# Gate/up projections of an f32 encoder on one core: a fourth seven-product pair per group, and the eight-product pairs' weight halves made by DMAs

## The chip, the cores and the metric

The kernel runs on one core of one Trainium2 chip. The metric is the device time of one execution in microseconds; several runs are summed up by their median. A core has TensorE (PE, matrix products), VectorE (DVE), ScalarE (ACT), GpSimd (POOL) and SyncE (SP). Each takes its own instructions strictly in order and waits on semaphores for the others. Loads from the chip's large memory (HBM) are DMAs: SP, ACT and POOL have a queue each, and all three share 16 DMA engines.

## The reference

A two-layer encoder over 256 tokens of width 2048, all in f32: in each layer a token mixer (spatial gating in the first, grouped-query attention in the second) with a memory attention beside it, an output projection, and a SwiGLU network. The change is in the last:

```python
def swiglu(h, w_gate_up, w_down):
    gate, up = jnp.split(h @ w_gate_up, 2, axis=-1)   # 2048 -> 2 x 5632
    return (jax.nn.silu(gate) * up) @ w_down          # 5632 -> 2048
```

## The kernel before

**Three passes per product.** TensorE multiplies in the rounded type F32R. To keep f32 accuracy each operand is split into an upper half, `hi` (the value rounded to F32R), and a lower half, `lo` (the value minus `hi`). One product of a 128-row slice of activations with a 128 x 512 block of weights is then three matmuls into the same PSUM bank: hi·hi, lo·hi and hi·lo (`matmul3`, lines 187 to 189). In the last the *weights'* lower half, tile `wlo`, is the moving operand. `halves` (line 265) makes a weight block's halves: ACT casts the loaded tile `raw` to `whi` (line 271), and DVE subtracts `whi` from `raw` into `wlo` (line 272). The pool has three buffers each for `whi` and `wlo`, used in turn, and four for `raw`.

**Pairs.** `Pair` (line 333) computes two 512-column blocks at once. For the gate/up projection these are a block of gate columns and the block of up columns that belongs to it; a group `f` of 11 in each layer is one such `Pair` object. The 2048 rows of the weights are eight *pairs* `i` of 256 rows. The two row slices, two token tiles and two column blocks of a pair make a 2 x 2 by 2 x 2 block product:

- `eight` does it with eight products, 24 matmuls, and needs the halves of four weight blocks (128 x 2048 in one tile);
- `seven` does it by a Strassen-like scheme with seven products, 21 matmuls. It needs sums of weights (tile `T`, three blocks, made by DVE on lines 371 to 373), the halves of seven blocks, and sums of activations (`feature_sums`, line 806), made once per layer and kept.

Products 1, 5, 6 and 7 occur in seven-product pairs alone; after the last of these `inner` (line 410 ff., the ACT copy of line 425 and the DVE adds of lines 426 to 428) combines them in tile `e`. Products 2, 3, 4 and 8 go on to the end of the group, when `outer` adds them to `e` with four DVE adds (line 448). Then ACT applies SILU (line 847) and the result is turned by DMA transposes for the down projection. In a layer's group 0 two of the eight pairs are seven-product pairs, in the other ten groups three, in the order 0, 3, 1, 4, 2, 5, 6, 7 with 0, 1 and 2 the seven-product ones.

**Order.** `run` (line 350) loads a pair (`fetch`, line 378; two DMAs of 512 KB on SP's queue) and starts its sums one pair ahead of its products. A scheduler then sets the final order of each engine's instructions, so matmuls of neighbouring pairs are interleaved. The down projection uses the same class with weights `w_down`.

## Time and profile before

| | |
|---|---|
| median of three runs | 1997.43 us (1996.91 to 1998.39) |
| the profiled execution | 2000.43 us |
| its span, first to last instruction | 1998.7 us |
| TensorE busy | 1987.4 us, 8956 matmuls |
| VectorE busy | 1595.2 us |
| ScalarE busy | 1228.9 us |
| GpSimd busy | 66.4 us |
| read from HBM | 394.45 MB |

The profile is of one execution. A row of a *group view* gives source line, engine, operation, output tile <- input tiles, form, count, then total busy time and mean ns of one, then the idle time just before them with what ended it. A row of *windows* gives a stretch of the span and, for each engine, busy us and instruction count (x), then the granted TensorE clock (1.00 is full), the mean busy share of the DMA engines (which goes a little over 1 when packets overlap) and GB/s. A row of *DMA issues* gives tile <- tensor, queue, count, size and median us from issue to landing.

### The profile page before, as it was taken

The numbers are of one execution on the slowest core, as the hardware profiler recorded it, in microseconds if no ns is written. First come the engines' busy times: TensorE is split into PE (matmuls) and PEld (weight loads), VectorE is DVE, ScalarE is ACT, GpSimd is POOL, SyncE is SP. The second block draws the span as 40 slices with busy tenths as digits, with TensorE's granted clock in tenths as the row PEclk, the third lists the DMA queues.
The fourth block names the chain that finished last, engine by engine and source line by source line (L and its number), as shares of the span: only waits on it lengthen the run. The fifth ranks groups of instructions, "written<-read, shape, count | busy, mean of one in ns | idle before, by whom it ended". The sixth has DMA issues, their size and how long they took to land.

```text
span 1998.7 us, 23974 instructions
## 1 busy us (share of the span) xinstructions
PE 1987.4 (99%) x8956; PEld 1646.0 (82%) x8956; DVE 1595.2 (80%) x1700; ACT 1228.9 (61%) x1476; POOL 66.4 (3%) x106
## 2 busy tenths in 40 slices
PE   9999999999999999999999999999999999999998
PEld 7888888888888878888888888888888888888887
DVE  6665568998888979886666886699988899888887
ACT  8757775676446764466765765756754466644673
POOL 2200001000000000000011000010000000000000
PEclk9999999999999999999999999999999999999999
DMA  9856875676656877657766434757866567765674
GB/s 352 296 187 179 242 212 188 190 231 216 220 197 183 229 201 229 205 184 232 228 219 201 162 129 158 219 180 207 241 205 212 188 206 213 225 219 190 199 220 139
DMA packets 276965, 416.48 MB, mean 208 GB/s; under 512 B 85200, under 2 KB 85456, under 8 KB 276848
## 3 DMA queue, kind: packets, MB, share of 16 engines
q1 hardware_dynamic: 199808, 387.62, 59.6%
q10 hardware_dynamic: 74352, 18.81, 5.8%
q0 software_dynamic: 2688, 8.52, 1.4%
q8 instruction: 70, 1.15, 0.2%
q14 instruction: 47, 0.39, 0.1%
HBM read 394.45 MB, written 2.10 MB: 198 GB/s over the span
## 4 chain that ended last, share of the span: by engine, by line
PE 89%; DVE 4%; DMA 3%; issue 2%; ACT 2%; SPq 0%; ACTq 0%; DVEq 0%
PE acc L189 26%; PE acc L187 26%; PE acc L188 26%; PE m L189 4%; PE m L187 4%; PE m L188 4%; DVE wlo L272 2%; DMA a<-a 1%; ACT whi L271 1%; DMA raw<-in_w_down 1%; DMA raw<-in_w_in_a 1%; PE m L193 1%; DVE T L371 0%; DVE e L448 0%; PE m L542 0%
## 5 line engine op out<-in xcount | busy, mean ns | idle before, releaser
L272 DVE TENSOR_TENSOR wlo<-raw,whi 128x2048 fp32r<-128x2048 f32 (+2 forms) x466 | 840.4, 1819 | 253.1 <-ACT whi L271 235.5
L271 ACT CAST whi<-raw 128x2048 fp32r<-128x2048 f32 (+2 forms) x466 | 705.6, 1535 | 428.5 <-PE acc L188 316.4
L187 PE MATMUL acc<-whi,h 128*128 128x512 f32 x1440 | 561.4, 390 | 0.8 <-ACT whi L271 0.8
L188 PE MATMUL acc<-whi,h 128*128 128x512 f32 x1440 | 561.0, 390 | 0.0
L189 PE MATMUL acc<-wlo,h 128*128 128x512 f32 x1440 | 516.0, 391 | 0.7 <-DVE wlo L272 0.6
L187 PE MATMUL acc<-whi,a 128*128 128x512 f32 x1052 | 410.0, 390 | 3.3 <-DVE x L448 2.1
L188 PE MATMUL acc<-whi,a 128*128 128x512 f32 x1052 | 410.0, 390 | 0.0
L189 PE MATMUL acc<-wlo,a 128*128 128x512 f32 x1052 | 394.4, 390 | 0.2 <-DVE wlo L272 0.2
L189 PEld LDWEIGHTS acc<-wlo,h 128*128 128x128 f32 x1440 | 270.4, 188 | 59.6 <-DVE wlo L272 4.1
L187 PEld LDWEIGHTS acc<-whi,h 128*128 128x128 f32 x1440 | 270.4, 188 | 56.5 <-ACT whi L271 1.5
L188 PEld LDWEIGHTS acc<-whi,h 128*128 128x128 f32 x1440 | 270.4, 188 | 55.7
L187 PEld LDWEIGHTS acc<-whi,a 128*128 128x128 f32 x1052 | 197.6, 188 | 44.7 <-issue 2.5
L189 PEld LDWEIGHTS acc<-wlo,a 128*128 128x128 f32 x1052 | 197.6, 188 | 42.3 <-DVE wlo L272 1.7
L188 PEld LDWEIGHTS acc<-whi,a 128*128 128x128 f32 x1052 | 197.6, 188 | 40.5
L271 ACT CAST whi<-T 128x1536 fp32r<-128x1536 f32 x84 | 124.4, 1481 | 96.3 <-PE acc L188 75.9
L272 DVE TENSOR_TENSOR wlo<-T,whi 128x1536 fp32r<-128x1536 f32 x84 | 146.9, 1749 | 0.0
L371 DVE TENSOR_TENSOR T<-raw 128x1024 f32<-128x1024 f32 x84 | 102.3, 1217 | 26.0 <-DMA raw<-in_w_gate_up 24.0
L189 PE MATMUL m<-wlo,a 128*128 128x512 f32 x272 | 106.1, 390 | 0.2 <-DVE wlo L272 0.2
L187 PE MATMUL m<-whi,a 128*128 128x512 f32 x272 | 106.0, 390 | 0.2 <-ACT whi L271 0.2
L188 PE MATMUL m<-whi,a 128*128 128x512 f32 x272 | 105.9, 389 | 0.0
L206 ACT COPY sg<-a 128x1024 uint16<-128x1024 uint16 x44 | 51.6, 1174 | 54.9 <-DMA a<-a 54.7
L200 ACT COPY a<-sg 128x1024 uint16<-128x1024 uint16 x44 | 45.9, 1044 | 26.0 <-issue 13.2
(122 smaller groups left out, 1474.7 us busy)
## 6 DMA issues: line engine op xcount, KB each, us to landing
raw<-in_w_gate_up SPq DMA_DIRECT2D x352, 512.0 KB, 4.7
raw<-in_w_down SPq DMA_DIRECT2D x176, 512.0 KB, 5.0
raw<-in_w_out SPq DMA_DIRECT2D x32, 1024.0 KB, 5.3
raw<-in_w_in_a SPq DMA_DIRECT2D x24, 1024.0 KB, 6.9
raw<-in_w_in_b SPq DMA_DIRECT2D x24, 1024.0 KB, 5.2
raw<-in_w_mem_kv SPq DMA_DIRECT2D x16, 1024.0 KB, 5.2
a<-in_mem_t POOLq DMA_DIRECT2D x16, 256.0 KB, 3.9
raw<-in_w_in_a SPq DMA_DIRECT2D x7, 512.0 KB, 8.1
```

What stands on the lines that cost most here:

```text
L187: nc.tensor.matmul(out, lhsT=a[0], rhs=b[0], start=start, stop=False)
L188: nc.tensor.matmul(out, lhsT=a[1], rhs=b[0], start=False, stop=False)
L189: nc.tensor.matmul(out, lhsT=a[0], rhs=b[1], start=False, stop=stop)
L193: nc.tensor.transpose(dst[:, c * P:(c + 1) * P], src[:, c * P:(c + 1) * P], ident)
L200: nc.scalar.copy(planes.rearrange("p (h n) -> p h n", h=2), src.bitcast(U16).rearrange("p (n h) -> p h n", h=2))
L206: nc.scalar.copy(halves, back.rearrange("p (h n) -> p n h", h=2))
L271: nc.scalar.copy(hi[:, cut], raw[:, cut])
L272: nc.vector.tensor_tensor(lo[:, cut], raw[:, cut], hi[:, cut].bitcast(F32), ALU.subtract)
L371: nc.vector.tensor_tensor(T[:, :2], raw[:, 1:4:2], w01, ALU.add)
```

## The change

- Every group but a layer's group 0 gets a fourth seven-product pair (pair 3), and seven- and eight-product pairs alternate: 0, 4, 1, 5, 2, 6, 3, 7 with 0 to 3 the seven-product ones. One more set of activation sums per layer is kept, so the room for activations grows from 26 to 29 tiles and `T` goes from two buffers to one, for the down projection's pairs too.
- In the gate/up groups (not in the down projection) an eight-product pair's halves are no longer made by ACT and DVE. Two casting DMAs on POOL's queue load the f32 weights straight into an F32R tile: that tile, one of the four `raw` buffers, is the upper half, and stays in use until the matmuls have read it. ACT writes its negative into a `wlo` buffer (two multiplications by -1, 128 x 1024 each), and two accumulating DMAs on POOL's queue load the same f32 weights from HBM a second time, added onto that negative.
- The matmuls that read the lower half come last in the pair (list `late`). The matmuls of gate/up and down pairs are now issued by `term` (line 405) instead of `matmul3`.

The core of the diff:

```diff
-FFN_TILES = 26
+FFN_TILES = 29
...
-                T = room["p"].tile([P, KC3, NB], F32, tag="T", name=nm("T"), bufs=2)
+                T = room["p"].tile([P, KC3, NB], F32, tag="T", name=nm("T"), bufs=1)
...
+        def block(self, i, n0):
+            return self.w[2 * i * P:(2 * i + 2) * P, n0:n0 + NB].rearrange("(c p) n -> p c n", p=P)
+
         def fetch(self, i):
-            raw = wp.tile([P, KC4, NB], F32, tag="raw", name=nm("raw"), bufs=RAW_TILES)
-            rows = slice(2 * i * P, (2 * i + 2) * P)
-            for cut, n0 in ((slice(1, 3), self.na), (slice(0, 4, 3), self.nb)):
-                nc.sync.dma_start(raw[:, cut], self.w[rows, n0:n0 + NB].rearrange("(c p) n -> p c n", p=P))
+            whole = i in self.fast or not self.dma
+            raw = wp.tile([P, KC4, NB], F32 if whole else F32R, tag="raw", name=nm("raw"), bufs=RAW_TILES)
+            for n, n0 in enumerate((self.na, self.nb)):
+                if whole:
+                    nc.sync.dma_start(raw[:, (slice(1, 3), slice(0, 4, 3))[n]], self.block(i, n0))
+                else:
+                    nc.gpsimd.dma_start(raw[:, 2 * n:2 * n + 2], self.block(i, n0))
             return raw
...
+        def term(self, name, a, b):
+            n = self.part[name] = self.part.get(name, 0) + 1
+            nc.tensor.matmul(self.bank[name], lhsT=a, rhs=b, start=n == 1, stop=n == 3 * self.of.get(name, self.most))
...
-            if self.bank:
+            if self.bank and not (self.dma and i == self.inmost):
                 inner, outer = inner[:2] + outer[:2], inner[2:] + outer[2:]
...
+        def eight_added(self, i, hi):
+            done = i == self.order[-1]
+            lo = wp.tile([P, KC4, NB], F32R, tag="wlo", name=nm("wlo"))
+            for n, n0 in enumerate((self.na, self.nb)):
+                cut = slice(2 * n, 2 * n + 2)
+                nc.scalar.mul(lo[:, cut], hi[:, cut].bitcast(F32), -1.0)
+                nc.gpsimd.dma_start(lo[:, cut], self.block(i, n0), accum_op=ALU.add)
+            late = {t: [] for t in range(NT)}
+            for n in range(2):
+                for t in range(NT):
+                    name = ((2, 3), (4, 8))[t][n]
+                    for c in range(2):
+                        self.add(name, self.parts.get(2 * i + c, t), (hi[:, 2 * n + c], lo[:, 2 * n + c]), late[t])
+                if not n:
+                    tick()
+            for t in range(NT):
+                for term in late[t]:
+                    self.term(*term)
+                if done:
+                    self.outer(t)
+            tick()
...
-        fast = (0, 1, 2)
+        fast = (0, 1, 2, 3)
...
-                order, some = ((3, 4, 5, 0, 6, 1, 7, 2), 2) if f == 0 else ((0, 3, 1, 4, 2, 5, 6, 7), 3)
-                pairs[f] = Pair(hF, sums, w_gate_up[l], f * NB, DFF + f * NB, order, fast[:some])
+                order, some = ((3, 4, 5, 0, 6, 1, 7, 2), 2) if f == 0 else ((0, 4, 1, 5, 2, 6, 3, 7), 4)
+                pairs[f] = Pair(hF, sums, w_gate_up[l], f * NB, DFF + f * NB, order, fast[:some], dma=True)
```

**Loading.** Before, all gate/up weights stand in SP's queue; here is a stretch in the first layer's second group. A row names the line, the tile that is written, the tensor that is read, the form, and the semaphores waited for: `DVE` until the tile's last reader is done.

```order
L380 DMA raw_489_2981<-in_w_gate_up 128x2x512 [waits DMAHW7_49,DMAHW6_49,DVE_49]
L380 DMA raw_489_2981<-in_w_gate_up 128x2x512
L380 DMA raw_494_3017<-in_w_gate_up 128x2x512 [waits DMAHW1_49,DMAHW0_49,DVE_49]
L380 DMA raw_494_3017<-in_w_gate_up 128x2x512
L380 DMA raw_499_3049<-in_w_gate_up 128x2x512 [waits DMAHW3_49,DMAHW2_49,DVE_49]
```

Now the eight-product pairs' loads stand in POOL's queue, which held no gate/up load before. Casting loads (line 385) and accumulating loads (line 441) take turns; the `raw` of the next eight-product pair but one stands ahead of the `wlo` of the next.

```order
L385 DMA raw_566_3505<-in_w_gate_up 128x2x512 [waits DMASW3_49,DMASW2_49,PE_49]
L385 DMA raw_566_3505<-in_w_gate_up 128x2x512
L441 DMA wlo_561_3468<-in_w_gate_up 128x2x512 [waits DMASW1_49,DMASW0_49,Activation_49]
L441 DMA wlo_561_3468<-in_w_gate_up 128x2x512 [waits Activation_49]
L385 DMA raw_586_3611<-in_w_gate_up 128x2x512 [waits DMASW7_49,DMASW6_49,PE_49]
L385 DMA raw_586_3611<-in_w_gate_up 128x2x512
L441 DMA wlo_577_3556<-in_w_gate_up 128x2x512 [waits DMASW5_49,DMASW4_49,Activation_49]
L441 DMA wlo_577_3556<-in_w_gate_up 128x2x512 [waits Activation_49]
```

A casting load now waits for PE, the last reader of its buffer, and an accumulating one for ACT's negative.

**The lower half's buffer.** Before, on PE, an eight-product pair in the same group: eight matmuls on `whi`, then the first that reads the lower half, which waits for DVE's subtraction.

```order
L187 MATMUL acc_541_3284<-whi_572_3478,h_418_2602 128x512 [waits Activation_49]
L188 MATMUL acc_541_3284<-whi_572_3478,h_419_2603 128x512
L187 MATMUL acc_542_3288<-whi_572_3478,h_418_2602 128x512
L188 MATMUL acc_542_3288<-whi_572_3478,h_419_2603 128x512
L187 MATMUL acc_543_3292<-whi_572_3478,h_423_2633 128x512
L188 MATMUL acc_543_3292<-whi_572_3478,h_424_2634 128x512
L187 MATMUL acc_548_3325<-whi_572_3478,h_423_2633 128x512
L188 MATMUL acc_548_3325<-whi_572_3478,h_424_2634 128x512
L189 MATMUL acc_541_3284<-wlo_573_3479,h_418_2602 128x512 [waits DVE_49]
```

Now the first lower-half matmul waits for an accumulating DMA. With three `wlo` buffers in turn and two of them taken by each seven-product pair, consecutive eight-product pairs of an alternating stretch get the *same* `wlo` buffer. The shortest distance that occurs is in the first layer where one group ends and the next begins: the row right ahead of this piece is the last that reads `wlo_803`, and the piece's last row is the first that reads `wlo_824`, which lies in the same buffer.

```order
L405 MATMUL acc_821_5142<-whi_815_5116,h_357_2155 128x512 [waits DVE_49]
L405 MATMUL acc_821_5142<-whi_815_5116,h_358_2156 128x512
L405 MATMUL acc_821_5142<-wlo_816_5117,h_357_2155 128x512
L405 MATMUL acc_821_5142<-raw_812_5109,h_401_2487 128x512
L405 MATMUL acc_821_5142<-raw_812_5109,h_402_2488 128x512
L405 MATMUL acc_821_5142<-raw_812_5109,h_401_2487 128x512
L405 MATMUL acc_821_5142<-raw_812_5109,h_402_2488 128x512
L405 MATMUL acc_825_5170<-raw_812_5109,h_401_2487 128x512 [waits DVE_49]
L405 MATMUL acc_825_5170<-raw_812_5109,h_402_2488 128x512
L405 MATMUL acc_825_5170<-raw_812_5109,h_401_2487 128x512
L405 MATMUL acc_825_5170<-raw_812_5109,h_402_2488 128x512
L405 MATMUL acc_819_5134<-wlo_824_5153,h_399_2464 128x512 [waits DMASW4_49]
```

Eleven matmuls stand between the two. Counted through the whole order of PE, there are 92 eight-product pairs in gate/up. In 80 of them the buffer was last read by another eight-product pair's lower-half matmuls; between that last read and the first matmul that needs the new lower half stand 11 to 17 matmuls in 10 cases (14.2 on average), 21 to 24 in 20 cases (22.35), 26 to 29 in 15 (27.5) and 31 to 41 in 35 (35.2). In the other 12 it was read by a seven-product pair, 39 to 72 matmuls earlier.

**ACT.** At the same group change ACT's order is as follows; `wlo_824`'s two multiplications stand behind the SILU of the group that ends.

```order
L440 ACTIVATE wlo_803_5054<-raw_792_5003 128x1024 [waits DMASW4_49,DMASW5_49,DMASW0_49,PE_49]
L440 ACTIVATE wlo_803_5054<-raw_792_5003 128x1024 [waits DMASW1_49]
L271 CAST whi_827_5186<-raw_822_5146 128x2048 [waits DMAHW2_49,DMAHW3_49,DVE_49,PE_49]
L884 ACTIVATE sg_810_5103<-e_800_5042,s1_426_2650 128x512 [waits DVE_49]
L884 ACTIVATE sg_811_5106<-e_800_5042,s1_429_2656 128x512 [waits DVE_49]
L271 CAST whi_829_5190<-T_823_5149 128x1536 [waits DVE_49,PE_49,Activation_49]
L440 ACTIVATE wlo_824_5153<-raw_812_5109 128x1024 [waits DMASW5_49,DMASW6_49,DMASW4_49,PE_49]
L440 ACTIVATE wlo_824_5153<-raw_812_5109 128x1024 [waits DMASW7_49]
```

Before, ACT's cast of a loaded block had nothing of the same block behind it but DVE's subtraction; now each multiplication is followed by a DMA that PE waits for.

More of the change, by code (lines that the diff above doesn't have):

```diff
@@ L333, in encoder, with __init__ @@
     class Pair:
-        def __init__(self, parts, sums, w, na, nb, order, fast, into=None):
+        def __init__(self, parts, sums, w, na, nb, order, fast, into=None, dma=False):
             self.parts, self.sums, self.w, self.na, self.nb, self.into = parts, sums, w, na, nb, into
             self.bank, self.two, self.part, self.ready = {}, {}, {}, {}
-            self.order, self.fast = order, fast
+            self.order, self.fast, self.dma = order, fast, dma
             some = [i for i in order if i in fast]
@@ L390, in add @@
                     self.bank[name] = psa.tile([P, NB], F32, tag="acc", name=nm("acc"))
-            self.part.setdefault(name, 0)
-            self.part[name] += 1
-            matmul3(self.bank[name], a, b, self.part[name] == 1, self.part[name] == self.of.get(name, self.most))
+            self.term(name, a[0], b[0])
+            self.term(name, a[1], b[0])
+            if late is None:
+                self.term(name, a[0], b[1])
+            else:
+                late.append((name, a[0], b[1]))
+        def term(self, name, a, b):
+            n = self.part[name] = self.part.get(name, 0) + 1
+            nc.tensor.matmul(self.bank[name], lhsT=a, rhs=b, start=n == 1, stop=n == 3 * self.of.get(name, self.most))
         def seven(self, i, raw, T):
@@ L409, in eight @@
         def eight(self, i, raw):
+            if self.dma:
+                return self.eight_added(i, raw)
             done = i == self.order[-1]
@@ L441, in add_inner, with outer @@
                 nc.vector.tensor_tensor(o.whole, o.whole, E[:, :2], ALU.add)
-        def outer(self, t):
+        def outer(self, t, some=(0, 1)):
             o = self.out
-            for n, name in enumerate(((2, 3), (4, 8))[t]):
+            for n in some:
+                name = ((2, 3), (4, 8))[t][n]
                 op = ALU.subtract if name == 4 and not self.into else ALU.add
```

2 lines of the change are left out of this document (1 added, 1 removed).

## Prediction

> **What bounds the kernel now.** I read the page's head first, then PE's waits, then windows of the gate/up stage, then DMA landings.
>
> ```profile
> span 1998.7 us, 23974 instructions
> PE 1987.4 (99%) x8956; PEld 1646.0 (82%) x8956; DVE 1595.2 (80%) x1700; ACT 1228.9 (61%) x1476; POOL 66.4 (3%) x106
> ```
>
> PE is busy for all but 11.3 us of the span. What it waits for, by the view of waits (engine, tile and line, releaser: us, times, longest):
>
> ```profile
> PE acc L187 <- DVE x L448: 2.1, 1, 2.1
> PE acc L187 <- ACT whi L271: 2.0, 3, 1.1
> PE acc L189 <- DVE wlo L272: 0.8, 3, 0.3
> ```
>
> Halves of weights keep PE waiting for 2.8 us in all, and no wait is longer than 2.1 us. So the kernel is bound by the number of matmuls: one fewer is worth its whole time, and any new wait of PE is paid in full. Two windows inside the first layer's gate/up groups, and the whole of that stretch:
>
> ```profile
> 360.00:400.00 40.00, 40.00 (x178) 33.11 (x177) 37.58 (x36) 26.21 (x23) 0.00 (x0) 1.00 0.74 214
> 400.00:440.00 40.00, 40.00 (x178) 33.14 (x177) 38.10 (x37) 27.43 (x23) 0.00 (x0) 1.00 0.72 219
> 280.00:460.00 180.00, 179.36 (x792) 147.53 (x792) 158.78 (x168) 119.24 (x121) 5.98 (x4) 1.00 0.68 208
> ```
>
> PE issues 178 matmuls in 40 us, 0.225 us each, at full clock. DVE is close behind with 38 of 40 us. The DMA engines are 0.68 to 0.74 busy and have slack; POOL has nothing to do.
>
> **Matmuls removed.** A seven-product pair has 21 matmuls and an eight-product one 24, so each of the 20 groups that get a fourth saves 3: 60 x 0.225 = **13.5 us**. A group goes from 183 matmuls (41.2 us) to 180 (40.5); a layer's group 0 keeps 186 (41.9). With PE as the bound this is all that can be gained here.
>
> **DVE and ACT.** These rows price the halves and sums:
>
> ```profile
> L272 DVE TENSOR_TENSOR wlo<-raw,whi 128x2048 fp32r<-128x2048 f32 x264 | 603.3, 2286 | 138.1 <-ACT whi L271 121.7 <-DMA raw<-in_w_down 15.5 <-DMA raw<-in_w_gate_up 0.9
> L271 ACT CAST whi<-raw 128x2048 fp32r<-128x2048 f32 x264 | 505.1, 1914 | 349.7 <-PE acc L188 253.8 <-DVE raw L372 36.5 <-PE m L188 20.9
> L272 DVE TENSOR_TENSOR wlo<-T,whi 128x1536 fp32r<-128x1536 f32 x84 | 146.9, 1749 | 0.0
> L271 ACT CAST whi<-raw 128x1024 fp32r<-128x1024 f32 x198 | 198.2, 1048 | 77.8 <-PE acc L188 62.6 <-DMA raw<-in_w_in_a 8.7 <-issue 6.3
> L271 ACT CAST whi<-T 128x1536 fp32r<-128x1536 f32 x84 | 124.4, 1481 | 96.3 <-PE acc L188 75.9 <-DVE T L373 13.3 <-DVE raw L372 7.0
> L371 DVE TENSOR_TENSOR T<-raw 128x1024 f32<-128x1024 f32 x84 | 102.3, 1217 | 26.0 <-DMA raw<-in_w_gate_up 24.0 <-DMA raw<-in_w_down 1.7
> L373 DVE TENSOR_TENSOR T<-raw 128x512 f32<-128x512 f32 x84 | 57.1, 681 | 0.1
> ```
>
> DVE loses five subtractions of 2.286 us per group and gains one seven-product pair, 2.286 + 1.749 + 1.217 + 2 x 0.681 = 6.6 us: 4.8 us less, about 33 of 40. ACT loses five casts of 1.914 and gains 1.914 + 1.481 and eight multiplications, each priced as the 128x1024 cast at 1.048: 2.2 us more, about 29 of 40. Neither becomes the bound by its busy time: 0. The single `T` buffer holds a pair's sums (2.6 us of DVE) back until DVE itself has read the last ones, and an eight-product pair of PE work (24 x 0.225 = 5.4 us) hides that; the fourth activation sum is made once per layer in DVE's slack: both 0, at worst 2.6 us per pair where the cover fails. `inner` and its four steps now come one eight-product pair, not three, before the group's end:
>
> ```profile
> L427 DVE TENSOR_TENSOR e<-m,e 128x1024 f32<-128x1024 f32 x32 | 38.9, 1216 | 0.0
> L428 DVE TENSOR_TENSOR e<-m,e 128x512 f32<-128x512 f32 x32 | 21.8, 683 | 0.2
> L426 DVE TENSOR_TENSOR e<-m,e 128x512 f32<-128x512 f32 x32 | 21.8, 682 | 0.0
> L425 ACT COPY e<-m 128x512 f32<-128x512 f32 x32 | 18.5, 577 | 0.0
> ```
>
> That is 3.2 us under 5.4 us of matmuls: 0, at worst 3.2 x 20 = 63 us.
>
> **DMA traffic.** Rows for what a transfer costs: a window at the start, where the queues are full, then transposes and loads in the gate/up stretch:
>
> ```profile
> 10.00:20.00 10.00, 10.00 (x45) 8.05 (x44) 9.49 (x17) 9.21 (x16) 0.00 (x0) 1.00 1.05 388
> ```
>
> ```profile
> q10 hardware_dynamic: 8448, 2.10, 7.6%
> ...
> raw<-in_w_gate_up SPq DMA_DIRECT2D x62, 512.0 KB, 4.7
> ...
> a<-a ACTq DMA_TRANSPOSE x8, 5.3
> ```
>
> Saturated, the engines move 388 GB/s, so a pair's weights (1.049 MB) take 2.70 us. Transposes took 7.6% of 180 us for eight, 1.7 us each, two per group. Before, a group is 8 x 2.70 + 3.4 = 25 us of DMA under 41.2 us of PE. After, the casting loads take over eight-product pairs' loads one for one (2.70; a cast was never timed here, and I price it as a copy). The accumulating loads are new: 1.049 MB per eight-product pair, read from HBM, added to what is read back from SBUF. Lower bound, a plain load: 2.70 us. Upper bound, the dearest DMA in the trace per byte: a transpose moves 2.10/8 = 0.26 MB in 1.7 us, so 6.8 us per pair. I take two reads, **5.40 us**, between them. Then a group needs 4 x 2.70 + 4 x 2.70 + 4 x 5.40 + 3.4 = 46.6 us of DMA against 40.5 of PE, a group 0 (six eight-product pairs) 57.4 against 41.9. By one read it would be 35.8 against 40.5. The Trainium skill, page "Collectives: The Full Stack", section "The bandwidth ceiling: the fold count and why AG ≠ RS ≠ AR", says that a reducing transfer is slowed by its two source reads, not by its addition, to half a copy's rate; no run shown so far has an accumulating DMA, so the trace neither agrees nor disagrees.
>
> **The new wait.** This decides. Consecutive eight-product pairs share one `wlo` buffer in 80 of 92 cases. The chain at each turn is: PE's last matmul on the old lower half, ACT's negative (1.048 us), the accumulating DMA from issue to landing (L), PE's first matmul on the new one. What PE has to do meanwhile are the matmuls counted in the order: 10 turns with 14.2 (3.20 us), 20 with 22.35 (5.03), 15 with 27.5 (6.18), 35 with 35.2 (7.91). Whatever 1.05 + L exceeds these is a PE wait. On ACT 4 of the group changes have the multiplication behind both SILUs of the ended group:
>
> ```profile
> L847 ACT ACTIVATE sg<-e,s 128x512 f32<-128x512 f32 x44 | 30.9, 720 | 15.7 <-DVE e L448 15.6
> ```
>
> That is 4 x 1.44 = 6 us more, between 0 and 32 (nine changes, with a cast and two adds too). POOL's queue: the accumulating load stands behind a casting one whose wait, for PE, is over earlier, so it isn't held; each issue costs POOL about 0.57 us by the first row here, at most twice that for twice the bytes, four per turn of 10 us.
>
> ```profile
> L594 POOL DMA_DIRECT2D a<-in_mem_t x16: 536/574/622, 37.3 to 1102.8; - x16
> DMA to landing us min/median/max: 3.1/3.9/9.4
> ```
>
> And L, by size and load, from the first 100 us, where the engines are full:
>
> ```profile
> raw<-in_w_in_a SPq DMA_DIRECT2D x12, 1024.0 KB, 11.1
> ...
> raw<-in_w_in_a SPq DMA_DIRECT2D x7, 512.0 KB, 8.1
> ...
> a<-in_mem_t POOLq DMA_DIRECT2D x8, 256.0 KB, 7.8
> ```
>
> 512 KB lands in 4.7 us at a share of 0.68 and in 8.1 us at about 1. With 46.6 us of DMA in a longer group the share comes out at 0.95 to 0.96 (20 x 46.6 + 2 x 57.4 = 1047 us of DMA in 20 x 40.5 + 2 x 41.9 + 196 of waits = 1090 us), and a straight line between the two rows gives **L = 7.6**. Bounds: 3.1 us, the quickest POOL landing, and 11.1, the largest median. At 7.6 the sum of waits is 10 x 5.45 + 20 x 3.62 + 15 x 2.47 + 35 x 0.74 = 190 us.
>
> **The sum.** 190 + 6 - 13.5 = +182 us. The profiled execution took 2000.43 us (span plus 1.7), 3.0 above the median of the runs, so 2000.4 + 182 - 3.0 = **2180 us**. For L from 6 to 10 the waits are 92 to 382 us, hence 2082 to 2398 us (the last with the 32). Chance 0.60.
>
> **Rivals.**
>
> *The accumulation is cheap.* If it reads back at no cost to the queues, the share stays near 35.8/40.5 = 0.88 and less, and L lies between 4.7 and 6: waits 40 to 92, time 2030 to 2082. For it: the engines have slack in the windows above. Against: every pair now sends 1 MB more. Chance 0.15.
>
> *The other side: faster.* The accumulating load lands before PE needs it at nearly all turns. Place: the 80 turns; price: up to 13.5 us, 1984 us. It decides from L = 2.9 on: there the ten shortest turns cost 7.5 us, which with the 6 us eats the gain; to win 4 us L must be 2.4 or less. Against it: the quickest 256 KB load of POOL took 3.1 us, and the quickest gate/up load of 512 KB 3.6 us (minimum, median and maximum of the 352):
>
> ```profile
> DMA to landing us min/median/max: 3.6/4.7/9.7
> ```
>
> For it: PE's order may leave slack at the turns that I count as tight, if ACT's negative starts earlier than I think. Faster 0.05, within 0.2% (what a measurement of this kernel can tell from no change) 0.05.
>
> *Far slower.* Accumulating in small pieces or casting could be several times a copy's cost, L above 10: at 11.1 the waits are 470 us, time 2460 us with the 6. Chance 0.10.
>
> *PE's clock falls in the waits.* The granted clock is 1.00 in every window here, but no PE wait so far passed 2.1 us; at L = 7.6 thirty turns wait 3.6 to 5.5 us. If the clock then halved for 15 matmuls, 3.4 us more would be lost each time: 30 x 3.4 = 101 us, 2281 us; for one matmul 7 us. The Trainium skill, "TensorE: Matmul & The Clock Gate", section "Why this matters for your kernels", warns that a gap of over about 3 us drops PE to half rate. By the sustained busy time of about 3.4 us that its Part 1 asks for the full rate, an estimate is 1.7 us per turn, 51 us. Chance 0.05, inside the range.
>
> **How the numbers follow.** Low end 2030: the cheap case's own low end. High end 2400: L = 10 with the 32 us. Inside: 0.60 + 0.15 + 0.05 = 0.80. Outside: 0.10 below, 0.10 above. Slower by over 0.2%: 0.60 + 0.15 + 0.10 + 0.05 = 0.90.
>
> **What would show it.** In the profile after: 8896 matmuls; PE busy far under 99%, with waits of L405 matmuls on `wlo` for DMAs from `in_w_gate_up` as the longest entry, about 80 times 2.5 us; accumulating loads landing in 6 to 10 us; a DMA share above 0.9 in gate/up windows; down-projection windows as before. Wrong if these loads land in under 4.7 us, if PE's waits name DVE, ACT or the casting loads instead, or if the lost time lies outside gate/up.

## The result, and the profile after

The changed kernel takes 2321.97 us (median of four runs, 2309.6 to 2328.67), the kernel before on the same chip 1997.91 us (four runs, 1996.91 to 2003.49). The ratio is 1.1608, with a 95% interval from 1.1555 to 1.1662: 16% slower. The profiled execution of the changed kernel took 2328.67 us, with a span of 2326.8 us, 328.1 us longer than the span of before.

The head of the page after, and from its slices the rows of TensorE's granted clock and of the DMA engines' busy share, in tenths:

```profile
span 2326.8 us, 24487 instructions
PE 2088.6 (90%) x8896; PEld 1677.8 (72%) x8896; DVE 1502.9 (65%) x1702; ACT 1265.0 (54%) x1590; POOL 420.9 (18%) x474
...
PEclk9999999999989999987999999999999899999889
DMA  9757899996899986998766446999967999869984
```

PE has 60 matmuls fewer, as foretold, and yet is busy for 101 us *longer* than before (1987.4 us). Outside that it is idle for 2326.8 - 2088.6 = 238.2 us, where it was 11.3 us: 227 us more. The two make the 328. The slices give a first hint: in all six slices in which PE's clock is below 9 the DMA row stands at 8 or 9, as it does in 25 of the 40.

PE's waits after (engine, tile and line, releaser: us, times, longest):

```profile
PE acc L405 <- DMA wlo<-in_w_gate_up: 163.4, 86, 5.6
PE m L405 <- ACT whi L271: 55.4, 16, 10.5
```

Two entries make up nearly all of it: the first lower-half matmul of an eight-product pair that waits for its accumulating DMA, 86 times, and, 16 times but up to 10.5 us long, the first product of a seven-product pair that waits for ACT's cast. The tensor's name in the first entry, `in_w_gate_up`, puts these waits into gate/up. Two rows of the groups agree. They are alike but for the second input: with `h` the first is of gate/up alone, and with `a` the second is of the down projection and of the gate/up products that use sums of activations:

```profile
L405 PE MATMUL acc<-wlo,h 128*128 128x512 f32 x904 | 304.2, 440 | 163.6 <-DMA wlo<-in_w_gate_up 163.4
L405 PE MATMUL acc<-wlo,a 128*128 128x512 f32 x688 | 254.5, 393 | 1.0 <-DVE wlo L272 1.0
```

Two of the windows that were shown for before (busy us and count of PE, PEld, DVE, ACT, POOL; clock, DMA share, GB/s), the landings of the two kinds of loads on POOL's queue, and the share of the 16 engines that each queue took of the span:

```profile
280.00:460.00 180.00, 160.62 (x659) 126.21 (x658) 109.48 (x143) 100.64 (x120) 57.81 (x62) 0.95 1.02 245
400.00:440.00 40.00, 30.66 (x117) 22.96 (x116) 21.64 (x25) 17.61 (x18) 10.17 (x11) 0.91 1.05 249
```

```profile
q0 software_dynamic: 102784, 201.48, 40.0%
q1 hardware_dynamic: 149760, 291.14, 37.5%
...
raw<-in_w_gate_up POOLq DMA_DIRECT2D x184, 512.0 KB, 8.9
wlo<-in_w_gate_up POOLq DMA_DIRECT2D x184, 512.0 KB, 7.6
```

In 400 to 440 us PE gets through 117 matmuls where it did 178. In the stretch of 280 to 460 us the DMA share went from 0.68 to 1.02: here the engines are full. That isn't so everywhere. Over the six stretches in which gate/up weights are loaded (277 to 496 us, 584 to 830, 899 to 1074, 1442 to 1666, 1752 to 1981, 2060 to 2249) the share is 1.01, 0.93, 0.92, 1.01, 0.96 and 0.91, where before it was 0.65 to 0.69. GB/s rose by less than the share (245 against 208), which suggests that an accumulated byte costs the engines more time than a copied one; "a plain second load" below tests it. The accumulating loads land in 7.6 us by the median, the quickest of the 184 in 5.6.

One turn in full, from the chain of work that ended last, between 400 and 432 us (start, us, what):

```profile
by line: DMA wlo<-in_w_gate_up 62.2%; issue 24.8%; PE acc L405 12.2%; ACT wlo L440 3.3%; POOL wlo L441 3.0%; DVE e L485 2.2%; POOLq L441 0.2%; ACT whi L271 0.1%; ACTq L440 0.1%; ACTq L271 0.1%
...
408.78 1.05 ACT wlo L440
409.83 0.30 issue
410.13 0.95 POOL wlo L441
411.07 7.58 DMA wlo<-in_w_gate_up
...
418.72 6.11 issue
...
424.85 6.59 DMA wlo<-in_w_gate_up
...
431.48 0.80 PE acc L405
```

Before, this stretch of the chain was PE matmuls from end to end. Now PE holds 12% of it: the chain runs through ACT's negative, POOL's issue and the transfer, and from there into the next one. What POOL waited for in the 6.11 us at 418.72 is ACT's next multiplication, and ACT was busy with something else, as its timeline shows (start, us, instruction, idle time before):

```profile
419.93 3.38 ACTq L201 DMA_TRANSPOSE a<-a  x1
423.49 2.01 ACT L440 ACTIVATE wlo<-raw 128x1024 fp32r<-128x1024 f32 x2 [3.59 <-issue]
```

ACT spent 3.38 us on issuing a DMA transpose, and the two multiplications stood behind it.

**The clock.** PE's timeline after that turn, and four short windows around it:

```profile
427.33 0.73 PE L405 MATMUL m<-whi,h 128*128 128x512 f32 x2 [1.98 <-ACT whi L271]
431.48 2.08 PE L405 MATMUL acc<-wlo,h 128*128 128x512 f32 x4 [3.42 <-DMA wlo<-in_w_gate_up]
```

```profile
418.00:424.00 6.00, 6.00 (x28) 4.98 (x27) 3.27 (x4) 1.56 (x2) 0.01 (x1) 1.00 1.16 350
427.40:431.40 4.00, 0.67 (x2) 0.23 (x2) 3.97 (x3) 4.00 (x5) 1.40 (x2) 0.84 0.97 162
431.40:435.40 4.00, 3.92 (x9) 3.14 (x10) 3.74 (x8) 0.52 (x2) 0.00 (x0) 0.50 1.13 305
437.00:441.00 4.00, 4.00 (x19) 3.27 (x19) 0.00 (x0) 1.41 (x2) 0.05 (x1) 1.00 0.48 161
```

PE stood still for 1.98 us, did two matmuls, stood still for 3.42 us; in the four microseconds after that the granted clock is 0.50, and 9 matmuls run instead of 18 or 19; from 437 on it is 1.00 again. The 0.84 of the second window shows that the clock had fallen before the wait was over: it is 1.00 from 427.4 to 430.1 us and 0.50 from 430.2 to 431.4, so it fell when PE had stood for some 2 us behind the two matmuls. This is where the longer *busy* time comes from. The mean clock over the span is 0.952, and (1 - 0.952) x 2326.8 us = 112 us. The Trainium skill, page "TensorE: Matmul & The Clock Gate", section "Why this matters for your kernels", names gaps of more than about 3 us as what sends PE back to half rate. These rows agree as to the half rate, but here the clock fell some 2 us into a gap, with two matmuls and a gap of 1.98 us ahead of it.

### The profile page after: what moved, and what is told of

Same layout as the page of the kernel before. It is cut to its first block, busy times and chain, and to the rows that moved or that the text cites. A ratio compares the mean times of both kernels' runs of the same rounds, so it can differ in the third digit from the quotient of the medians.

```text
span 2326.8 us, 24487 instructions
## 1 busy us (share of the span) xinstructions
PE 2088.6 (90%) x8896; PEld 1677.8 (72%) x8896; DVE 1502.9 (65%) x1702; ACT 1265.0 (54%) x1590; POOL 420.9 (18%) x474
## 3 DMA queue, kind: packets, MB, share of 16 engines
q1 hardware_dynamic: 149760, 291.14, 37.5%
## 4 chain that ended last, share of the span: by engine, by line
PE 56%; DMA 22%; issue 10%; ACT 5%; DVE 4%; POOL 2%; ACTq 1%; SPq 0%; DVEq 0%; POOLq 0%
PE acc L405 27%; DMA wlo<-in_w_gate_up 14%; PE acc L189 7%; PE acc L187 7%; PE acc L188 7%; DMA a<-a 5%; PE m L405 4%; DVE wlo L272 2%; DMA raw<-in_w_gate_up 2%; ACT wlo L440 2%; ACT whi L271 2%; POOL wlo L441 1%; DMA raw<-in_w_in_a 1%; ACTq L201 1%; ACT a L200 1%
## 5 line engine op out<-in xcount | busy, mean ns | idle before, releaser
L272 DVE TENSOR_TENSOR wlo<-raw,whi 128x1024 fp32r<-128x1024 f32 (+2 forms) x374 | 630.9, 1707 | 415.1 <-ACT whi L271 263.4
L271 ACT CAST whi<-raw 128x1024 fp32r<-128x1024 f32 (+2 forms) x374 | 528.5, 1439 | 355.9 <-PE acc L405 119.4
L405 PE MATMUL acc<-wlo,h 128*128 128x512 f32 x904 | 304.2, 440 | 163.6 <-DMA wlo<-in_w_gate_up 163.4
L405 PE MATMUL acc<-whi,a 128*128 128x512 f32 x1376 | 412.3, 393 | 3.6 <-ACT whi L271 2.6
L405 PE MATMUL acc<-raw,h 128*128 128x512 f32 x1472 | 383.1, 398 | 0.0
L441 POOL DMA_DIRECT2D wlo<-in_w_gate_up x184 | 226.2, 1359 | 719.5 <-ACT wlo L440 718.1
L405 PEld LDWEIGHTS acc<-wlo,h 128*128 128x128 f32 x904 | 178.6, 207 | 240.7 <-DMA wlo<-in_w_gate_up 206.9
L405 PEld LDWEIGHTS acc<-raw,h 128*128 128x128 f32 x1472 | 284.8, 194 | 61.8
L405 PEld LDWEIGHTS acc<-whi,a 128*128 128x128 f32 x1376 | 261.0, 190 | 61.0 <-ACT whi L271 3.9
L385 POOL DMA_DIRECT2D raw<-in_w_gate_up x184 | 146.3, 853 | 769.4 <-DVE wlo L272 514.2
L440 ACT ACTIVATE wlo<-raw 128x1024 fp32r<-128x1024 f32 x184 | 184.6, 1050 | 153.9 <-PE acc L405 145.9
L405 PE MATMUL acc<-wlo,a 128*128 128x512 f32 x688 | 254.5, 393 | 1.0 <-DVE wlo L272 1.0
L405 PE MATMUL m<-whi,a 128*128 128x512 f32 x664 | 216.1, 408 | 5.0 <-ACT whi L271 3.1
L272 DVE TENSOR_TENSOR wlo<-T,whi 128x1536 fp32r<-128x1536 f32 x104 | 182.2, 1752 | 13.4 <-ACT whi L271 11.2
L187 PE MATMUL acc<-whi,h 128*128 128x512 f32 x416 | 162.5, 392 | 0.7 <-ACT whi L271 0.7
L188 PE MATMUL acc<-whi,h 128*128 128x512 f32 x416 | 162.2, 390 | 0.0
L405 PEld LDWEIGHTS m<-whi,a 128*128 128x128 f32 x664 | 130.7, 198 | 36.9 <-ACT whi L271 7.0
L405 PEld LDWEIGHTS acc<-wlo,a 128*128 128x128 f32 x688 | 130.8, 190 | 30.2 <-DVE wlo L272 2.6
L188 PE MATMUL acc<-whi,a 128*128 128x512 f32 x384 | 149.8, 391 | 0.0
```

Source lines behind the costliest of these rows:

```text
L187: nc.tensor.matmul(out, lhsT=a[0], rhs=b[0], start=start, stop=False)
L188: nc.tensor.matmul(out, lhsT=a[1], rhs=b[0], start=False, stop=False)
L271: nc.scalar.copy(hi[:, cut], raw[:, cut])
L272: nc.vector.tensor_tensor(lo[:, cut], raw[:, cut], hi[:, cut].bitcast(F32), ALU.subtract)
L385: nc.gpsimd.dma_start(raw[:, 2 * n:2 * n + 2], self.block(i, n0))
L405: nc.tensor.matmul(self.bank[name], lhsT=a, rhs=b, start=n == 1, stop=n == 3 * self.of.get(name, self.most))
```

## The experiments

Two theories say why the waits are so long. **Turn-around**: a lower half's buffer comes free too late, and the chain from PE's last read to PE's next first read is longer than the matmuls that lie between. **Full engines**: the accumulating loads bring more DMA work than the 16 engines can do beside PE's work, so whatever is arranged, PE ends up waiting for bytes. A third, **the clock**, says that a good part of the time isn't waiting at all but half speed after the waits. A fourth was put to the test only in the mixed runs further down: **the landing**, by which an accumulating load keeps PE waiting even when the engines have slack. Each run below is compared with runs of the kernel before on the same chip.

### Turns apart

The lower halves are put into `wlo` and `whi` buffers by turns, so that more matmuls lie between two uses of a buffer: 38 at least and 57 on average, by the buffers' addresses in the built program, instead of 22 and 34.

```diff
-            lo = wp.tile([P, KC4, NB], F32R, tag="wlo", name=nm("wlo"))
+            turn[0] += 1
+            tag = ("wlo", "whi")[turn[0] % 2]
+            lo = wp.tile([P, KC4, NB], F32R, tag=tag, name=nm("wlo"))
```

> The lower halves of consecutive eight-product pairs are allocated in turn from the wlo and the whi buffers, with nothing else changed; from the last read of a buffer to the first need of the new lower half PE then has 38 matmuls at least and 57 on average (22 and 34 in the changed kernel). Theory T (the turn-around of the buffer: old lower half read, negative, accumulating load, new one needed): 57 x 0.225 = 12.8 us is longer than 1.05 + 7.6 us, so waits on wlo for DMAs fall from 163 us to under 40, the clock stays near 1.00, time 2000 to 2070 us. Theory D (the DMA engines are full: 46.6 us of transfers per group against 40.5 us of PE): the stage still takes 1047 us instead of 911, time 2130 us or more, with waits spread over all loads.

Measured: 2196.02 us, ratio 1.0954 (1.0882 to 1.1027). Its waits, a window and the landing:

```profile
PE acc L407 <- DMA wlo<-in_w_gate_up: 84.4, 60, 2.9
PE m L407 <- ACT whi L271: 55.6, 24, 8.2
...
280.00:460.00 180.00, 161.98 (x678) 128.46 (x677) 115.97 (x150) 103.16 (x123) 62.59 (x66) 0.96 1.04 256
...
wlo<-in_w_gate_up POOLq DMA_DIRECT2D x184, 512.0 KB, 10.7
```

That is outside what the turn-around expects (2000 to 2070 us) and inside what full engines do. The turn-around is worth 133 of the 324 us. In the changed kernel ACT stood still for 145.9 us, 29 times, ahead of its multiplications until PE had read a buffer; here it is 26.3 us, 6 times. But 191 us stay, with the engines at 1.04 here and at 0.97 to 1.06 over the six stretches of gate/up loads: the loads start earlier and in return take 10.7 us instead of 7.6, as they would behind other transfers, and not for a late start.

### A plain second load

The second load without its addition: the same bytes are read from HBM and written over ACT's negative, so the lower half holds the weights themselves.

```diff
-                nc.gpsimd.dma_start(lo[:, cut], self.block(i, n0), accum_op=ALU.add)
+                nc.gpsimd.dma_start(lo[:, cut], self.block(i, n0))
```

> The second load overwrites the negative with a plain casting load in place of the accumulating one: same bytes from HBM, same queue, same order; the lower half then holds the rounded weights, so the products are not the reference's. If accumulating reads twice (two-read theory): the DMA time of software queue packets falls from 930 to about 610 us, landing from 7.6 to 5.5 us, waits on wlo from 163 to under 60 us, time 2040 to 2130 us. If the addition is free: landing stays at 7.6 us and the time at 2310 to 2330 us.

Measured: 2168.68 us, ratio 1.0818 (1.0761 to 1.0874).

```profile
q0 software_dynamic: 102784, 201.48, 32.9%
...
wlo<-in_w_gate_up POOLq DMA_DIRECT2D x184, 512.0 KB, 4.6
...
PE m L405 <- ACT whi L271: 62.5, 21, 8.1
```

POOL's queue has the same packets and bytes as in the changed kernel and takes 32.9% of 2163.0 us instead of 40.0% of 2326.8: 712 us instead of 931. The addition alone costs 219 us of engine time, and about half of the loss. That is less than a second read of the same length would cost: expected were 610 us and a time of 2040 to 2130 us. The waits on `wlo` fell from 163.4 to 42.3 us, inside what was expected, but the waits on `whi` stayed, at 62.5 us.

### Filler matmuls

Ten matmuls with weights of zero ahead of each eight-product pair's lower-half matmuls, 920 in all, to keep PE going where it would wait.

```diff
+            for _ in range(10):
+                nc.tensor.matmul(self.bank[2][:64], lhsT=zero, rhs=hi[:, 0], start=False, stop=False)
```

> Ten matmuls with a zero weight tile are put in front of each eight-product pair's lower-half matmuls: 920 more matmuls, about 207 us of PE work at full clock, that add nothing to the result. If the clock falls because PE stands still (clock theory): the granted clock goes back to 0.99 or more, the filler lies in the waits, and the time falls by 40 to 110 us to 2210 to 2280 us although there is more work. If the clock is not the cause: the filler fills the waits at best, time 2320 us, or up to 2320 + 207 us where it does not.

Measured: 2405.6 us, ratio 1.2 (1.194 to 1.206), so the expectation of the clock theory, 2210 to 2280 us and a clock of 0.99, was missed: the time rose, and the mean clock is 0.965 where it was 0.952. The fillers are 920 x 0.225 = 207 us of work. Idle time fell from 238.2 to 167.9 us (span 2407.8, PE busy 2239.9). The busy time beyond the work at full clock fell from 114 to 2239.9 - 1974.2 - 207 = 59 us (1974.2 us is what the changed kernel's 8896 matmuls take at full clock, from the next run). So the slower matmuls cost half as much, and the fillers still cost more than they saved. The scheduler also set many other matmuls in another order here (the waits on `whi` fell from 55.4 to 5.6 us), so this run is no clean measure of the clock's share.

### No second load

The accumulating loads are left out and nothing else; the lower half is then ACT's negative of the upper half.

```diff
-                nc.gpsimd.dma_start(lo[:, cut], self.block(i, n0), accum_op=ALU.add)
```

> The accumulating loads are left out; the lower half is the negative of the upper one, so the products are not the reference's. Casting loads, order and everything else stay. Both theories of the second load (turn-around and full engines) expect the loss to go: wlo waits for ACT alone, DMA per group 25 us, time 1984 to 2000 us. A rival, that the casting loads on the software queue cost by themselves: landing of raw stays near 8.9 us and PE waits for raw, time above 2050 us.

Measured: 1992.31 us, ratio 0.9937 (0.9915 to 0.996).

```profile
PE 1974.2 (99%) x8896; PEld 1635.5 (82%) x8896; DVE 1493.3 (75%) x1702; ACT 1262.3 (63%) x1590; POOL 190.4 (10%) x290
...
q0 software_dynamic: 52736, 105.00, 18.5%
```

This is the clearest run of the study: one line out, and 330 us are gone. The order, the casting loads, ACT's multiplications and the single `T` buffer together cost nothing, and the 60 matmuls are worth what was foretold (1974.2 - 1987.4 = -13.2 us of PE). **The whole loss belongs to the accumulating loads**, that is to the second load and its addition together; by the run before, the loads without the addition still cost about half of it.

It also prices the loads. 18.5% of 1990.5 us is 368 us on POOL's queue; some 25 us of it are other loads (1.2% of 2116.2 us with the order alone, below, where this queue has no gate/up load), so the casting loads take 343 us / 92 pairs = 3.73 us a pair. The plain second loads take 712 - 368 = 344 us, 3.73 us a pair. The accumulating ones take 931 - 368 = 563 us, **6.12 us a pair, 1.64 times** a load without addition. At this price a pair's accumulating loads are 6.12 us of work for all 16 engines even when nothing else is under way. The Trainium skill, page "Collectives: The Full Stack", section "The bandwidth ceiling: the fold count and why AG ≠ RS ≠ AR", gives the reducing step of a collective half of a copy's rate, for its two reads; here, with an accumulating load into SBUF, the factor was 1.64 and not 2.

### The order alone

The new order and the fourth seven-product pair, but the halves made by ACT and DVE as before (`dma=True` taken out of the call).

> The fourth seven-product pair and the alternating order alone: all weights are loaded and halved as in the kernel before. DVE theory: DVE then has 4 x 6.6 + 4 x 2.29 + 7.3 = 42.9 us per group against 40.5 of PE, so DVE becomes the bound in 20 groups and the kernel is 20 to 60 us slower than before. Rival (DVE has slack enough in the groups' other parts): 13 us faster than before.

Measured: 2118.04 us, ratio 1.0569 (1.0542 to 1.0595): 115 us over before, where at most 60 were expected.

```profile
PE m L405 <- ACT whi L271: 53.3, 37, 4.4
...
280.00:460.00 180.00, 167.38 (x716) 130.99 (x715) 153.48 (x172) 110.39 (x117) 2.29 (x4) 1.00 0.62 187
```

So with these buffers a fourth seven-product pair can't be had in the old way: the DMA halves are what makes room for it, and the second load is what spoils it. The DMA engines have slack (0.62), and DVE isn't full either: 153.48 of 180 us, where before it was 158.78. PE waits for ACT and DVE and what lies between them. Which of them, the next runs ask.

### Two T buffers, and four whi buffers

Both on top of the order alone; in both a `raw` buffer is given up for the room, so each measures two changes at once.

```diff
-RAW_TILES = 4
+RAW_TILES = 3
...
-                T = room["p"].tile([P, KC3, NB], F32, tag="T", name=nm("T"), bufs=1)
+                T = room["p"].tile([P, KC3, NB], F32, tag="T", name=nm("T"), bufs=2)
```

> The run of the alternating order alone, with two buffers for T again, as before the change, and three for raw instead of four to make room. If the single T buffer is what makes the alternating order 115 us slower than before, the time falls to 0 to 30 us above before. If it is the three whi and wlo buffers, of which a seven-product pair takes two each, that are given back by PE too late for ACT's next cast, it stays at 95 to 140 us above before.

```diff
-        hi = wp.tile([P, KC4, NB], F32R, tag="whi", name=nm("whi"))[:, :n]
+        hi = wp.tile([P, KC4, NB], F32R, tag="whi", name=nm("whi"), bufs=4)[:, :n]
```

> The run of the alternating order alone, with four buffers for whi instead of three, and three for raw instead of four to make room. If ACT's wait for a whi buffer that PE still reads (241 us of idle time of ACT, 89 times) is what delays the seven-product pairs' casts, the waits of PE on whi fall from 53 us to under 20 and the time to 30 to 70 us above before. If T or the sums of DVE hold them, it stays at 95 to 140 us above before.

Measured: 2081.76 us with two `T` (ratio 1.039, 1.037 to 1.0411), 2110.15 us with four `whi` (1.0537, 1.0512 to 1.0562). The second `T` gives back 36 us, between the two expectations; the fourth `whi` 8, as its second expectation says. PE's waits with two `T` buffers:

```profile
PE acc L405 <- DVE wlo L272: 25.5, 31, 1.8
PE m L405 <- DVE wlo L272: 13.3, 15, 2.2
PE m L405 <- ACT whi L271: 9.4, 11, 2.8
```

The waits on `whi` went from 53.3 to 9.4 us, and DVE is now what PE waits for most. So about a third of the 115 us was the single `T`. What the other 78 us are wasn't shown. DVE has more to do, 6.6 us for a seven-product pair where an eight-product one gave it 2.3, 4.3 us more in each of 20 groups while PE's own work shrinks; but it is busy for 156 of the 180 us from 280 to 460, no more than before. The short chain between ACT and DVE may be as much of it.

### Apart and plain

Turns apart and a plain second load at once (both edits above).

> Both cures together: lower halves of consecutive eight-product pairs apart, and the second load plain instead of accumulating (the lower half then holds the rounded weights, so the products are not the reference's). Full-engine theory with the prices measured now (3.1 us per pair through SP, 3.7 cast, 3.7 second load, 3.9 of transposes per group): 46.1 us of DMA per group, which full engines (share 1.07) pass in 43.1 us against 40.5 of PE: 40 to 70 us over the kernel before. If the turn-around were the only cause: 13 us under the kernel before. If the second load as such (issue, semaphores, POOL) holds PE up: as with one cure, 160 us over.

Measured: 2090.38 us, ratio 1.0431 (1.0399 to 1.0462). Neither remedy alone takes the time down as far. But 87 us over before stay, more than the 40 to 70 that full engines give and less than the 160 of the third expectation, so none of the three was met; that the turn-around is the only cause is ruled out.

```profile
PE m L407 <- ACT whi L271: 56.6, 16, 8.8
PE acc L407 <- DMA wlo<-in_w_gate_up: 12.3, 18, 1.9
...
280.00:460.00 180.00, 170.94 (x744) 139.09 (x742) 127.36 (x161) 112.81 (x133) 50.98 (x72) 0.99 1.00 286
```

The wait on `wlo` is nearly gone, the wait on `whi` is not, and the engines still stand at 1.00. ACT's timeline ahead of this run's longest wait (8.8 us, PE goes on at 464.8) shows who holds the cast:

```profile
461.79 1.16 ACT L206 COPY sg<-a 128x1024 uint16<-128x1024 uint16 x1 [10.45 <-DMA a<-a]
462.85 1.89 ACT L271 CAST whi<-raw 128x2048 fp32r<-128x2048 f32 x1
```

ACT stands for 10.45 us in the copy behind a DMA transpose of the activations, and the cast that PE needs is next in its queue. The longest such stand is 11.4 us in the changed kernel, 11.2 with turns apart, 10.2 with the plain second load and 10.4 here; it is 4.6 us in the kernel before and 6.6 us without the second load. So with much DMA work a small transfer that has nothing to do with weights can hold PE up as well.

### No wait for the transposes

The changed kernel, with that copy reading the tile ahead of the transpose.

```diff
-            nc.scalar.copy(halves, back.rearrange("p (h n) -> p n h", h=2))
+            nc.scalar.copy(halves, (planes if over else back).rearrange("p (h n) -> p n h", h=2))
```

> The changed kernel, but the copies behind the DMA transposes read the tile ahead of the transpose instead of the one behind it: the transposes still run and load the engines, but no copy on ACT waits for them any more. The kernel then multiplies untransposed activations in these places, so its output is not the reference's. If the waits of PE on whi (58 us in the changed kernel, some of 7 to 10 us) come from ACT standing in a copy that waits for a transpose slowed by full DMA engines, they fall under 15 us, and the time falls by these 45 us and about half as much again of lowered clock: 2230 to 2285 us. If the full engines set the time anyhow, the waits on whi go but the waits on wlo grow by as much, and the time stays at 2300 to 2335 us. If the whi waits come from whi buffers or late loads, they stay over 40 us.

Measured: 2322.84 us, ratio 1.1597 (1.1527 to 1.1667): no change against the changed kernel's 1.1608.

```profile
PE acc L405 <- DMA wlo<-in_w_gate_up: 183.8, 89, 13.8
PE m L405 <- ACT whi L271: 27.8, 11, 6.7
```

The waits on `whi` halved, from 55.4 to 27.8 us, and those on `wlo` rose by 20.4. ACT's stand behind the transposes was the cause of half of the `whi` waits (the expectation was all but 15 us), and taking it away bought nothing: what PE gained at one wait it lost at the next. The time is the one that the full-engine theory expected.

### Two of four, one of four

The DMA halves for two of a group's four eight-product pairs (4 and 6), or for one (5), and none in a layer's group 0; the others by ACT and DVE; buffers as in "turns apart".

```diff
-                pairs[f] = Pair(hF, sums, w_gate_up[l], f * NB, DFF + f * NB, order, fast[:some], dma=True)
+                pairs[f] = Pair(hF, sums, w_gate_up[l], f * NB, DFF + f * NB, order, fast[:some], dma=(4, 6) if f else ())
```

> Of the four eight-product pairs of a group only two (4 and 6) get their halves by DMAs, in buffers taken in turn; the others, and all of group 0, by ACT and DVE. DMA per group 42 us, passed in 39 by full engines; DVE 38.3 us of 40.5. Full-engine theory with the clock: waits only at the shortest turns, time between 15 us under and 25 us over the kernel before. If any accumulating load costs PE a wait by its landing alone: 40 waits of 2.5 us, 80 us over or more.

> As the run with two, but only pair 5 of each group gets its halves by DMAs. DMA 36 us per group, DVE 40.6 of 40.5 us. Full-engine theory: no waits on wlo DMAs; DVE is now the tight engine: from 13 us under to 15 us over the kernel before. If accumulating loads cost PE a wait each: 20 x 2.5 us, 40 us over.

Measured: 2132.16 us, ratio 1.0633 (1.061 to 1.0657), and 2138.46 us, ratio 1.0671 (1.0641 to 1.0701). The window, the landings and PE's wait with one of four:

```profile
280.00:460.00 180.00, 167.44 (x719) 133.63 (x718) 148.61 (x169) 110.22 (x118) 11.70 (x14) 0.99 0.69 199
...
wlo<-in_w_gate_up POOLq DMA_DIRECT2D x40, 512.0 KB, 7.8
...
PE acc L407 <- DMA wlo<-in_w_gate_up: 28.1, 20, 3.2
```

Both times lie far over what the full-engine theory expected, at most 25 and 15 us over before; 129 and 135 were measured. Much of that is what this order costs by itself ("the order alone"), which neither expectation had in it. But the waits on `wlo` are against the theory too, which had few of them or none. The landing theory, a wait for each accumulating load, is nearer: PE waits 49 times for 40 pairs (71.4 us) and 20 times for 20 (28.1 us), though 1.4 to 1.5 us and not 2.5 each. The engines have slack (0.77 and 0.69 in the window of 280 to 460 us), yet the accumulating loads land in 8.1 and 7.8 us, no sooner than in the changed kernel: at 6.12 us of engine time for a pair, such a load can fill the engines for most of that time by itself. So neither mix pays: the order's own cost stays, and each accumulating load still brings a wait.

### The old order with the DMA halves

The DMA halves stay, order and number of seven-product pairs are those of before: three of them, and five eight-product pairs by DMA.

```diff
-                order, some = ((3, 4, 5, 0, 6, 1, 7, 2), 2) if f == 0 else ((0, 4, 1, 5, 2, 6, 3, 7), 4)
+                order, some = ((3, 4, 5, 0, 6, 1, 7, 2), 2) if f == 0 else ((0, 3, 1, 4, 2, 5, 6, 7), 3)
```

> The DMA halves stay, the fourth seven-product pair and the alternation go: three seven-product pairs per group in the order of before, five eight-product pairs by casting and accumulating loads. If full DMA engines set the time, a group needs 3 x 3.14 + 5 x (3.7 + 6.1) + 3.9 = 62 us of DMA instead of 56, some 1386 us in all, and at the share of 1.08 that the changed kernel reached the stage takes about 1280 us instead of 908: 2380 us, 2330 to 2430, slower than the changed kernel. If the alternating order is a large part of the loss (it costs 115 us without the DMAs), the time falls under the changed kernel's: 2200 to 2290 us.

Measured: 2340.38 us, ratio 1.1697 (1.1647 to 1.1746), inside what full engines give and well above the other expectation.

```profile
q0 software_dynamic: 124544, 243.43, 47.5%
...
wlo<-in_w_gate_up POOLq DMA_DIRECT2D x224, 512.0 KB, 9.1
```

Without the new order the kernel is no faster. The run changes two things at once, though: 112 pairs by DMA instead of 92 put 1085 us on POOL's queue (47.5% of 2336.8 us, less the 25 of other loads) where the changed kernel has 906. So it doesn't show that the order costs nothing beside accumulating loads; that the order is free beside the casting loads is shown by "no second load".

### The clock, over all runs

The changed kernel and its variants have the same 8896 matmuls, 1974.2 us at full clock, except for "the old order" with its 8956 and "filler matmuls", which has 920 more and is left out. What PE's busy time is above that, against PE's idle time: 114 to 238 us in the changed kernel, 66 to 149 with turns apart, 64 to 125 with the plain load, 50 to 92 with the order alone, 30 to 82 with both remedies, 100 to 241 without the transposes' wait. In all of these, and in the four not listed, each microsecond of waiting came with another 0.36 to 0.54 us of slower matmuls (with the old order 122 to 228, against 1987.4 us). The mean clock accounts for nearly all of it in the changed kernel (112 of 114 us), for 52 of 66 us with turns apart, and not everywhere: with the order alone the mean clock of 0.989 stands for 23 us of the 50. What the other 27 are stays open.

## Why the prediction was right, and where it was not

The direction, the place and the mechanism held: slower, in gate/up, by waits of L405 matmuls on `wlo` for accumulating DMAs. The time lies 142 us above the forecast of 2180 us and inside its range of 2030 to 2400 us. That it lies inside is in part luck: the range was drawn from L and the cost of the addition, and what filled it was the clock and the waits on `whi`, of which neither set a bound. By its steps:

- **Matmuls removed, -13.5 us**: -13.2 us of PE busy and a ratio of 0.9937 without the second load. Right.
- **DVE, ACT, the single T, `inner`: 0.** Right for this change: the same run carries them all at no cost. The cover is thin, though. Where DVE still makes the eight-product pairs' halves, a second `T`, at the price of a `raw` buffer, gives back 36 us.
- **DMA traffic, 46.6 us a group.** Too low. The casting loads were priced 2.70 us a pair and took 3.73, the accumulating ones 5.40 and took 6.12, SP's loads 2.70 and took 3.14 (37.5% of 2326.8 us for 291.14 MB). With these a group needs 4 x (3.14 + 3.73 + 6.12) + 3.4 = 55 us of DMA against 40.5 of PE. The share came out near the forecast 0.95 to 0.96 (0.91 to 1.01 over the six stretches) only because the groups grew as the work did. So the engines are a second limit beside the turn-around, which shows when the turns are taken apart, and the prediction had only the one. The profile of before could have told. The prediction's own 25 us of DMA under 41.2 us of PE is a share of 0.61, and its windows show 0.68 to 0.74. The row just above the one that it took for the transposes prices SP's loads in this very stretch, 60.3% of 180 us for 35.17 MB, 3.24 us a pair:

```profile
q1 hardware_dynamic: 18236, 35.17, 60.3%
```

- **L = 7.6 us.** Measured 7.6 us, but the agreement is luck. The straight line ran through landings of plain loads and made L depend on the mean share alone. At 0.69 it gives 4.8 us; "one of four" had 7.8 us there, and its plain casting loads 4.7. With full engines L was 10.7 us (turns apart), and no accumulating load of the changed kernel landed in under 5.6 us. So the addition's own engine time is in L, and the line left it out. And L isn't all of the load: a turn also has 0.30 us between ACT and POOL and 0.95 us of POOL's issue in it, and the four issues of a turn are two casting ones of 0.74 us and two accumulating ones of 1.23 us, not 0.57 us each:

```profile
L441 POOL DMA_DIRECT2D wlo<-in_w_gate_up x184: 1194/1232/2145, 297.5 to 2246.4; - x184
```

- **The turns.** The count of shared buffers was wrong, in the section on the change and in the prediction. The pool doesn't give its buffers strictly in turn: by the addresses in the built program, which no trace shows, 53 and not 80 of the 92 eight-product pairs get the buffer of the eight-product pair before, and `wlo_824` does not lie in the buffer of `wlo_803` but in one that a seven-product pair had. The distances are then 22 to 72 matmuls, 34 on average, and the prediction's own sum with them gives 135 us of waits at L = 7.6 instead of 190. Measured were 163 us on `wlo` in 86 waits. The trace shows ACT held by PE's reads ahead of 29 multiplications only, so at most of the turns another link of the chain came last.
- **ACT behind SILU, 6 us.** No run measures this term. What the traces show ahead of ACT's instructions are the DMA transposes, in their issue (3.38 us in the turn above) and in the copies that wait for them. The waits on `whi`, 55.4 us, were not foreseen at all; "no wait for the transposes" traces half of them to these copies.
- **The sum, 190 + 6 - 13.5 = +182 us.** This is the step that failed. The waits grew by 227 us and not by 196, which is near only because 27 us too much on `wlo` stood against 55 us on `whi` that weren't in the sum. And the sum had no term for the clock: the matmuls took 114 us more than at full clock. The prediction had it as a rival with a chance of 0.05, at 101 us. It was no rival: its own list has thirty turns that wait 3.6 to 5.5 us, longer than any wait seen before, and in the runs the slower matmuls came with the waits, so the term belongs *in* the sum. With it the forecast would have been the 2281 us that stand there.
- **The other rivals.** *The accumulation is cheap*, *faster* and *far slower* are out: the landing is 7.6 us, and an accumulating load takes 1.64 times a plain one of engine time.

What stays open is how the 191 us that are left with turns apart divide between full engines and the landing of each load. Full engines fit that run and the old order with the DMA halves; the mixed runs show waits without them. Each remedy shifts the waits (apart and plain: 87 us left; without the transposes' wait: nothing gained). No version that makes the reference's products was found that beats the kernel before.

## What to carry to other kernels

Moving work from compute engines to DMAs pays only while the DMA engines have slack in that very stage: add up the engine time per stage, with prices from that stage's own rows and an accumulating load at 1.6 times a plain one, before looking at who waits for whom. Where the sum is over the compute engine's time, better buffers take off part of the loss (133 of 324 us here) and not the rest. And a forecast of waits on a TensorE that ran without a gap should have a term for slower matmuls: here about half a microsecond for each one of waiting.

## What the runs showed of the hardware

- TensorE's granted clock fell to 0.50 some 2 us into a wait of 3.42 us that followed a wait of 1.98 us and two matmuls, and it was still 0.50 over the four microseconds of work behind the wait.
- Accumulating DMAs took 6.12 us of the 16 engines for 1.05 MB, casting loads on POOL's queue 3.73, first and plain second ones alike, SP's loads 3.14 (means over whole runs, under the load of those runs). POOL took 1.23 us to issue one accumulating DMA of 512 KB and 0.74 us to issue a casting one.
- With few accumulating loads and the engines at 0.69 these still landed in 7.8 us; a plain second load landed in 4.6 us at 0.98 (both shares from 280 to 460 us).
- DMA transposes of activations landed in 6.2 us by the median and 19.9 at most in the changed kernel, in 5.4 and 10.0 before. ACT's copies of `sg` that wait for them stood for 91.6 us (54.7 before), the longest 11.4 us (4.6 before):

```profile
ACT sg L206 <- DMA a<-a: 91.6, 26, 11.4
```
